# A hybrid decoder trunk: two weight products computed as 2x2 block products in seven multiplications, with the weight sums added up in DRAM

## The chip, the core and the metric

The kernel runs on one core of a Trainium2 chip. The metric is the device time of one execution in microseconds (us). One core has a matrix engine (TensorE, called PE in the profile, with its weight loads as PEld), a vector engine (VectorE, DVE), an activation engine (ScalarE, ACT), a general engine (GpSimd, POOL) and a queue engine (SyncE, SP) which here only starts transfers (DMAs). Each engine works through its own instructions in order and waits on semaphores for the others.

## The reference, cut to what matters

One layer on 512 tokens of width 1024. `h @ W_in` gives the inputs of three branches (a state-space model, a short convolution, a sliding-window attention) and three gates. The part that the change touches comes after them:

```python
merged = (g0 * (y_ssm @ w_branch[0]) + g1 * (y_conv @ w_branch[1]) + g2 * (y_attn @ w_branch[2]))
x = x + merged @ w_out                                    # 1024 x 1024
hf = rms_norm(x, norm_ffn) @ w_ffn_in                     # 1024 x 5632
x = x + (silu(hf[..., :2816]) * hf[..., 2816:]) @ w_ffn_out   # 2816 x 1024
pg = sigmoid(rms_norm(x, norm_ple) @ w_ple_gate)
x = x + pg * (p @ w_ple_proj)
return rms_norm(x, norm_final)
```

All of it is float32. Every product is computed as three products of split numbers: an operand is a high part (`hi`, rounded to the matrix engine's float32r) plus a rest (`lo`), and hi*hi + hi*lo + lo*hi are added up in PSUM.

## The kernel before, in words

**Weight stream.** Every weight matrix is cut into slabs of at most 128x2048 numbers (1 MB), in the order in which they are used. `emit_load` (L179) starts the DMA of a slab on SP into one of two `raw` buffers. A slab has two halves of 1024 columns; `emit_split` (L187) makes a half ready: ACT copies it to `hi` (L206), DVE subtracts to get `lo` (L207, issued up to LAG = 4 ticks later). The halves go round a ring of slots (`hla`, four of them). From the `w_out` stage on the ring has seven slots (`hlb` adds three, L1201). `take` and `group` say which half is wanted now, `retire` that one has been used; both split ahead as far as the ring allows.

**Clock of the program.** `pump()` is called after each triple of matmuls; one call is a tick. `later(d, f)` issues work d ticks on, so that the vector engines' work is put between matmuls. The order on every engine is fixed by this program order; there is no scheduler.

**Stages.** First the start (norm, `p @ w_ple_proj`), then `z_tile` products (8 K-blocks x 3 matmuls of 512 columns for each 128 output columns), the attention beside the convolution, then gates and branch products with the state-space model (SSM) in the background: `ssm_gen` runs four channel tiles, each a chain over PE, ACT, DVE, POOL and small DMAs through DRAM (`su`, `sy`). POOL multiplies in it (L1050, L1063, L1111), and in the convolution (L925 to L929). Then `branch(..., 2)` finishes `merged` tile by tile and splits it into `mh`, `ml` (`split_ap`, L243).

**[token, d] products.** `td_gemm` (L1230) multiplies `merged` by `w_out` and the FFN's hidden tiles by `w_ffn_out`, in three chunks of 8, 8 and 6 hidden tiles (`CHUNKS`, L161). `td_outer_k` (L1218) holds four PSUM banks for the four token tiles and goes over the K-blocks: one weight half serves 2 K-blocks x 4 token tiles x 3 = 24 matmuls. `accum` (L1209) adds each finished bank to the residual `xr`. With a norm behind it (after `w_out` and after the last chunk) the second column half is done token tile by token tile, and `Norm.pre` (L1253) queues square, rstd (POOL), scale (DVE) and the transposes of that tile. The FFN chunks before the products are `z_tile`s: two SiLU tiles and two gating tiles for each pair of hidden tiles, split into `gh`, `gl` (L1320).

The 512 tokens are four tiles of 128; `w_out` has 8 K-blocks, the FFN chunks 8, 8 and 6.

Of the kernel before, what the change touches and what calls it, by code (L numbers as in the profile page):

```python
# [25 lines left out]
WARM = 3  # L26
PREP_RATE = 1.7
# [48 lines left out]
def hybrid_trunk_kernel(  # L76
# [44 lines left out]
    def add_slab(ap, k, n, axis):  # L121
        s = len(slabs)
        slabs.append(dict(ap=ap, k=k, n=n, raw=None))
        cnt = 2 if k * n == 2048 else 1
        for i in range(cnt):
            halves.append(dict(s=s, i=i, cnt=cnt, axis=axis, hl=None))
# [31 lines left out]
    for n in range(2):  # L158
        for kk in range(2):
            add_slab(kn(w_out[0][kk * 512:kk * 512 + 512, n * 512:n * 512 + 512]), 4, 512, "k")  # L160
    CHUNKS = [(0, 8), (8, 8), (16, 6)]  # L161
    for h0, hn in CHUNKS:
        for j in range(h0, h0 + hn, 2):
            for ab in range(2):
                c0 = ab * FFN + j * 128
                add_slab(kn(w_ffn_in[0][:, c0:c0 + 256]), 8, 256, "n")
        for n in range(2):
            for k0 in range(0, hn, 4):
                kq = min(4, hn - k0)
                r0 = (h0 + k0) * 128  # L170
                add_slab(kn(w_ffn_out[0][r0:r0 + kq * 128, n * 512:n * 512 + 512]), kq, 512, "k")
# [5 lines left out]
    state = dict(pump=0, delay=False, split=0, load=0, next=0, top=3, slot=0, pools=[hla] * 4)  # L177

    def emit_load():  # L179
        s = slabs[state["load"]]  # L180
        state["load"] += 1
        t = rawp.tile([128, 2048], F32, tag="raw", name="raw")
        v = t[:, 0:s["k"] * s["n"]].rearrange("p (k n) -> p k n", k=s["k"])
        sp.dma_start(out=v, in_=s["ap"])
        s["raw"] = v

    def emit_split():  # L187
# [5 lines left out]
        k, n, i = s["k"], s["n"], h["i"]  # L193
        if h["cnt"] == 1:
            src = s["raw"]
        elif h["axis"] == "n":
            n //= 2
            src = s["raw"][:, :, i * n:(i + 1) * n]
        else:
            k //= 2  # L200
            src = s["raw"][:, i * k:(i + 1) * k, :]
        pl = state["pools"][state["slot"] % len(state["pools"])]
        state["slot"] += 1
        hi = pl.tile([128, 1024], F32R, tag="hi", name="hi").rearrange("p (k n) -> p k n", k=k)
        lo = pl.tile([128, 1024], F32R, tag="lo", name="lo").rearrange("p (k n) -> p k n", k=k)
# [60 lines left out]
    def pump(tick=True):  # L266
        if tick:
            state["pump"] += 1
            run_due(state["pump"])
# [117 lines left out]
    def prep_gen(tp):  # L387
        # per-channel vectors: ssm_d (4 tiles) and the conv taps (3 x 4 tiles)
# [59 lines left out]
    def prep_fine(tp, lt, ldt, T1, T2, tabs):  # L448
# [73 lines left out]
        # coefficients  # L522
# [85 lines left out]
    # the tensor engine's clock rises only under load  # L608
# [293 lines left out]

    fine.append(dict(gen=attn_fine(), rate=1, credit=0))
# [52 lines left out]
    # chunks of 4 tokens; channels of a group pair and the time in the chunk share the partitions  # L956
    def ssm_gen(ct):
# [69 lines left out]
        # the two row halves of the array write to banks of their own  # L1027
# [117 lines left out]
    def branch(d0, sgs, yh, yl, mode, mh=None, ml=None):  # L1145
        hl = take()
        for i in range(2):
# [8 lines left out]
            if mode == 2:  # L1156
                split_ap(merged[:, d], mh[:, d], ml[:, d])
# [29 lines left out]
    mst = ExitStack()  # L1187
    mhp = open_pool(mst, "mhl", side="right")
    mh = mhp.tile([128, KD, T], F32R, tag="mh", name="mh")
    ml = mhp.tile([128, KD, T], F32R, tag="ml", name="ml")  # L1190
    sg1 = gates()
    branch(0, sg0, yfh, yfl, 2, mh, ml)
    branch(2, sg1, yfh, yfl, 2, mh, ml)
    for d0 in (4, 6):
        branch(d0, gates(), yfh, yfl, 2, mh, ml)
# [7 lines left out]
    state["slot"] = 4  # L1203
# [14 lines left out]
    def td_outer_k(ah, al, kn_, n):  # L1218
        pss = [ps_z() for _ in range(4)]
        for h in range(kn_ // 2):  # L1220
            hi, lo = take()
            for t in range(4):
                for k in range(2):
                    kk = 2 * h + k
                    td_mm(pss[t], ah, al, kk, slice(t * 128, (t + 1) * 128), hi, lo, k, kk == kn_ - 1)
                    pump()
        for t in range(4):
            accum(t, n, pss[t])

    def td_gemm(ah, al, kn_, pre_fn=None):  # L1230
        td_outer_k(ah, al, kn_, 0)
        if pre_fn is None:
            td_outer_k(ah, al, kn_, 1)
            return
        nh = kn_ // 2
        h0 = group(nh)
        for t in range(4):
            ahead()
            ps = ps_z()
            for kk in range(kn_):  # L1240
                hi, lo = halves[h0 + kk // 2]["hl"]
# [180 lines left out]
```

## Time and profile before

| | |
|---|---|
| median of three runs | 894.33 us (893.93 to 896.04) |
| span of the profiled execution, first to last instruction | 892.6 us |
| around the span, to the median of the runs | 1.7 us |
| PE / DVE / ACT / POOL busy | 874.4 / 491.1 / 341.0 / 95.9 us |
| bytes moved by DMA | 107.25 MB |

The page gives the profiled execution no time of its own beside its span. PE's busy time counts overlapped matmuls once; the length shown for a matmul (about 390 ns for 512 columns) is its way through the array, and the distance of two starts is what one costs. "Idle before" is the time that an engine stood still ahead of an instruction, with what released it.

### The profile page before, as it was taken

To read this page: it belongs to the slowest core of one execution; us is meant where nothing else is said; L and a number is where in the kernel's file an instruction comes from. 1 tells how busy PE (TensorE), PEld (TensorE's weight loads), DVE (VectorE), ACT (ScalarE), POOL (GpSimd) and SP (SyncE) were. 2 spreads that over 40 slices of the span, in tenths; PEclk is the share of its full clock that TensorE was granted. 3 is DMA by queue.
4 is the path that set the end of the run, shared out by engine and by line. 5 is a ranking of instruction groups with operands and counts; after the bars stand their busy time and mean duration, and the time that the engine had idled before them with its cause. 6 is when DMAs were issued, how large, how long until landed. Compare 5 with 4: busy or idle time off the path is not lost.

```text
span 892.6 us, 10527 instructions
## 1 busy us (share of the span) xinstructions
PE 874.4 (98%) x4143; PEld 715.2 (80%) x4143; DVE 491.1 (55%) x737; ACT 341.0 (38%) x546; POOL 95.9 (11%) x86
## 2 busy tenths in 40 slices
PE   8999999999999979999999999999999999999997
PEld 6988787877777758888889888888888888888886
DVE  3789698948588585554545433333333333334654
ACT  5665556445443343433334322212222212222533
POOL 1030061713123030000000000000000000000000
PEclk9999999999999989999999999999999999999998
DMA  8756511253634523223813322222225332233002
GB/s 300 216 189 218 195 59 30 66 173 113 178 95 156 156 94 107 95 79 134 284 46 107 130 94 95 95 95 94 95 95 211 99 100 87 72 120 110 29 1 94
DMA packets 84849, 107.25 MB, mean 120 GB/s; under 512 B 6120, under 2 KB 66176, under 8 KB 84288
## 3 DMA queue, kind: packets, MB, share of 16 engines
q1 hardware_dynamic: 84800, 106.59, 36.5%
q8 instruction: 32, 0.52, 0.2%
q14 instruction: 17, 0.14, 0.1%
HBM read 94.83 MB, written 11.55 MB: 119 GB/s over the span
## 4 chain that ended last, share of the span: by engine, by line
PE 77%; DVE 10%; issue 4%; ACT 3%; DMA 3%; SPq 1%; POOL 1%; POOLq 0%; DVEq 0%; ACTq 0%
PE z L248 17%; PE z L249 16%; PE z L250 16%; PE z L1216 8%; PE z L1215 8%; PE z L1214 8%; DVE lo L207 1%; DVE s_t L839 1%; DMA xt<-in_x_dram 1%; PE t L325 1%; DVE s_t L812 1%; DMA raw<-in_w_in_dram 1%; POOL gsw L1063 1%; ACT s_t L826 1%; PE t L1084 1%
## 5 line engine op out<-in xcount | busy, mean ns | idle before, releaser
L248 PE MATMUL z<-h,hi 128*128 128x512 f32 (+1 forms) x776 | 298.6, 385 | 0.0
L207 DVE TENSOR_TENSOR lo<-raw,hi 128x1024 fp32r<-128x1024 f32 x142 | 177.6, 1253 | 216.2 <-ACT hi L206 216.1
L249 PE MATMUL z<-l,hi 128*128 128x512 f32 (+1 forms) x776 | 292.2, 377 | 0.0
L250 PE MATMUL z<-h,lo 128*128 128x512 f32 (+1 forms) x776 | 292.1, 376 | 0.0
L206 ACT CAST hi<-raw 128x1024 fp32r<-128x1024 f32 x142 | 148.2, 1047 | 133.1 <-PE z L1216 87.2
L248 PEld LDWEIGHTS z<-h,hi 128*128 128x128 f32 x776 | 146.8, 189 | 29.9 <-issue 3.7
L250 PEld LDWEIGHTS z<-h,lo 128*128 128x128 f32 x776 | 146.7, 189 | 27.6
L249 PEld LDWEIGHTS z<-l,hi 128*128 128x128 f32 x776 | 147.0, 189 | 24.7
L1214 PE MATMUL z<-hi,gh 128*128 128x512 f32 x176 | 69.5, 395 | 0.0
L1216 PE MATMUL z<-hi,gl 128*128 128x512 f32 x176 | 69.1, 393 | 0.0
L1215 PE MATMUL z<-lo,gh 128*128 128x512 f32 x176 | 69.1, 392 | 0.0
L1265 POOL TENSOR_TENSOR rs<-ms,nhalf 128x1 f32<-128x1 f32 x8 | 4.4, 550 | 487.2 <-DVE ms L1264 487.2
L244 ACT CAST gh<-sil 128x512 fp32r<-128x512 f32 x22 | 13.6, 620 | 86.0 <-DVE sil L1319 86.0
L248 PE MATMUL z<-yh,hi 128*128 128x512 f32 x112 | 45.1, 403 | 0.0
L249 PE MATMUL z<-yl,hi 128*128 128x512 f32 x112 | 44.2, 395 | 0.1
L250 PE MATMUL z<-yh,lo 128*128 128x512 f32 x112 | 44.2, 395 | 0.0
L1310 ACT ACTIVATE sil<-z 128x512 f32<-128x512 f32 x22 | 13.2, 598 | 75.4 <-PE z L250 75.4
L1319 DVE TENSOR_TENSOR sil<-z,sil 128x512 f32<-128x512 f32 x22 | 15.2, 691 | 46.8 <-PE z L250 46.8
L1216 PEld LDWEIGHTS z<-hi,gl 128*128 128x128 f32 x176 | 33.1, 188 | 7.5
L1215 PEld LDWEIGHTS z<-lo,gh 128*128 128x128 f32 x176 | 33.1, 188 | 7.4
L1214 PEld LDWEIGHTS z<-hi,gh 128*128 128x128 f32 x176 | 33.1, 188 | 7.3
L1211 DVE TENSOR_TENSOR xr<-z,xr 128x512 f32<-128x512 f32 x32 | 21.5, 687 | 15.6 <-PE z L1216 15.5
(258 smaller groups left out, 1058.5 us busy)
## 6 DMA issues: line engine op xcount, KB each, us to landing
raw<-in_w_in_dram SPq DMA_DIRECT2D x23, 1024.0 KB, 5.5
raw<-in_w_ffn_in_dram SPq DMA_DIRECT2D x22, 1024.0 KB, 5.2
raw<-in_w_ffn_out_dram SPq DMA_DIRECT2D x10, 1024.0 KB, 5.0
raw<-in_w_branch_dram SPq DMA_DIRECT2D x12, 512.0 KB, 3.4
cs<-tb SPq DMA_DIRECT2D x4, 1024.0 KB, 5.2
raw<-in_w_out_dram SPq DMA_DIRECT2D x4, 1024.0 KB, 5.8
raw<-in_w_ple_gate_dram SPq DMA_DIRECT2D x4, 1024.0 KB, 5.1
xt<-in_x_dram SPq DMA_DIRECT2D x4, 512.0 KB, 9.4
```

The costliest lines, as they stand in the source:

```text
L206: act.copy(out=hi, in_=src)
L207: todo = [lambda: dve.tensor_tensor(lo, src, hi.bitcast(F32), ALU.subtract)]
L244: act.copy(out=hi, in_=src)
L248: pe.matmul(ps, wh, ah, start=first, stop=False)
L249: pe.matmul(ps, wh, al, start=False, stop=False)
L250: pe.matmul(ps, wl, ah, start=False, stop=last)
L1211: dve.tensor_tensor(dst, ps, dst, ALU.add)
L1214: pe.matmul(ps, ah[:, kk, ts], hi[:, k, ns], start=(kk == 0), stop=False)
L1215: pe.matmul(ps, ah[:, kk, ts], lo[:, k, ns], start=False, stop=False)
L1216: pe.matmul(ps, al[:, kk, ts], hi[:, k, ns], start=False, stop=last)
L1310: act.activation(out=s, in_=ps, func=AF.Silu)
L1319: dve.tensor_tensor(sil[i], ps, sil[i], ALU.mult)
```

## The change

`w_out` and each of the three chunks of `w_ffn_out` are taken as 2x2 block products: tokens in two halves of 256, K-blocks in two interleaved halves (even and odd), output columns in two halves of 512. Instead of eight block multiplications there are seven (Strassen's scheme in Winograd's form), each 256 tokens x `kt` K-blocks x 512 columns, with `kt` = 4, 4, 4 and 3. Products that share terms go on adding into the same PSUM bank after it has been read, and each product is added to, or subtracted from, one quarter of `xr`.

*Left sides.* `forms` builds, for a pair of hidden (or merged) tiles, four sums on DVE and splits seven forms of 2x256 or 256 columns into `fh`, `fl`. These take 28 KB a partition each; the ring has four slots instead of seven until the last stage, and `gh`, `gl`, `mh`, `ml` are gone.

*Right sides.* Three of the seven are blocks of the weights, four are sums (`t1` to `t4`), built in DRAM beforehand: per block product eight DMAs on POOL's queue, four copies and four with an add, 1 MB each (0.75 MB in the last chunk), 32 in all. They are issued one every 16 ticks from the start of the attention on; a load that needs them issues what is still missing first.

The gain for the last norm and `pp` (`ppt`) are now loaded when the last stage begins, in a place that the forms left.

```diff
-    for n in range(2):
-        for kk in range(2):
-            add_slab(kn(w_out[0][kk * 512:kk * 512 + 512, n * 512:n * 512 + 512]), 4, 512, "k")
+    A11, A12, A22, FD, S2, S3, S4 = range(7)
+    ORDER = (A11, FD, S2, S4, S3, A12, A22)
+    ORDER_NORM = (A11, FD, S2, S4, A12, S3, A22)
+    def add_block_product(w, r0, kt, order):
+        def blk(h, n):
+            v = w[r0:r0 + 2 * kt * 128, n * 512:n * 512 + 512].rearrange("(i h p) n -> h p i n", h=2, p=128)
+            return v[h]
+        t1, t2, t3, t4 = (dram.tile([128, kt, 512], F32, tag=f"T{len(sums)}_{i}", name="T") for i in range(4))
+        ops = []
+        def op(dst, src, add=False):
+            ops.append(lambda: pool.dma_start(out=dst, in_=src, **(dict(accum_op=ALU.add) if add else {})))
+        op(t1, blk(0, 1))
+        op(t3, blk(0, 1))
+        op(t1, blk(0, 0), True)
+        op(t3, blk(1, 1), True)
+        op(t2, t1)
+        op(t2, blk(1, 1), True)
+        op(t4, t2)
+        op(t4, blk(1, 0), True)
+        sums.append(ops)
+        right = {A11: blk(0, 0), A12: blk(1, 0), A22: t4, FD: t1, S2: t2, S3: t3, S4: blk(1, 1)}
+        for f in order:
+            add_slab(right[f], kt, 512, "k", 16 if len(sums) < 3 else 32)
+    add_block_product(w_out[0], 0, 4, ORDER_NORM)
...
+    for i in (0, 2):
+        sum_ops.extend(f for two in zip(sums[i], sums[i + 1]) for f in two)
     def emit_load():
...
+        while n_sum - len(sum_ops) < s["need"]:
+            sum_ops.popleft()()
...
     def pump(tick=True):
         if tick:
             state["pump"] += 1
+            if state["sums"] and sum_ops and state["pump"] % SUM_EVERY == 0:
+                sum_ops.popleft()()
...
+    def forms(g, i):
+        sums = fmp.tile([128, 4, 256], F32, tag="sums", name="sums")
+        g11, g12, g21, g22 = (g[:, h, o:o + 256] for o in (0, 256) for h in range(2))
+        split_ap(g[:, :, 0:256], fh[:, 0:2, i], fl[:, 0:2, i])
+        dve.tensor_tensor(sums[:, 0], g21, g22, ALU.subtract)
+        dve.tensor_tensor(sums[:, 1], sums[:, 0], g11, ALU.subtract)
+        dve.tensor_tensor(sums[:, 2], g11, g21, ALU.subtract)
+        dve.tensor_tensor(sums[:, 3], g12, sums[:, 1], ALU.add)
+        split_ap(sums, fh[:, 3:7, i], fl[:, 3:7, i])
+        split_ap(g22, fh[:, 2, i], fl[:, 2, i])
...
-    hlb = open_pool(ctx, "hlb", 3)
-    state["pools"] = [hla] * 4 + [hlb] * 3
...
+    PRODUCTS = {A11: (0, True, 1, 0, 0), FD: (1, True, 1, 1, 1), S2: (0, False, -1, 0, 1), S4: (1, False, 1, 0, 1),
+                S3: (0, False, -1, 1, 1), A12: (2, True, 1, 0, 0), A22: (0, False, 1, 1, 0)}
+    def block_product(kt, norm=None):
+        banks = {}
+        for i, f in enumerate(ORDER if norm is None else ORDER_NORM):
+            bk, first, sign, th, n = PRODUCTS[f]
+            if first:
+                banks[bk] = [(ps_t if bk == 2 else ps_z)() for _ in range(2)]
+            for q in range(2):
+                h0 = group(1)
+                if q == 0:
+                    ahead()
+                hi, lo = halves[h0]["hl"]
+                k0, kc = halves[h0]["part"][0:2]
+                for t in range(2):
+                    ps, ts = banks[bk][t], slice(t * 128, (t + 1) * 128)
+                    for k in range(kc):
+                        kk = k0 + k
+                        st = first and kk == 0
+                        last = kk == kt - 1
+                        pe.matmul(ps, fh[:, f, kk, ts], hi[:, k], start=st, stop=False, skip_group_check=True)
+                        pe.matmul(ps, fl[:, f, kk, ts], hi[:, k], start=False, stop=False, skip_group_check=True)
+                        pe.matmul(ps, fh[:, f, kk, ts], lo[:, k], start=False, stop=last, skip_group_check=True)
+                        pump()
+                    if last:
+                        dst = xr[:, 2 * th + t, n * 512:(n + 1) * 512]
+                        dve.tensor_tensor(dst, ps if sign > 0 else dst, dst if sign > 0 else ps,
+                                          ALU.add if sign > 0 else ALU.subtract)
+                        if norm is not None and i in (4, 6):
+                            norm.pre(2 * th + t)
+                retire(h0)
...
-    td_gemm(mh, ml, 8, nf.pre)
+    block_product(4, nf)
...
-                split_ap(sil[i], gh[:, j + i], gl[:, j + i])
+            forms(g, j // 2)
+        block_product(hn // 2, npl if ci == 2 else None)
```

## Rows read from the trace of the kernel before

**Rows 1.** The page: busy time by engine, clock and DMA in 40 slices.
```profile
PE 874.4 (98%) x4143; PEld 715.2 (80%) x4143; DVE 491.1 (55%) x737; ACT 341.0 (38%) x546; POOL 95.9 (11%) x86
PEclk9999999999999989999999999999999999999998
DMA  8756511253634523223813322222225332233002
```
**Rows 2.** Busy time by stretch; columns PE, PEld, DVE, ACT, POOL, clock, DMA share, GB/s.
```profile
200.00:250.00 50.00, 50.00 (x242) 39.06 (x241) 34.81 (x41) 25.47 (x41) 15.08 (x10) 1.00 0.45 133
300.00:350.00 50.00, 45.23 (x201) 34.30 (x200) 30.47 (x38) 16.42 (x24) 7.53 (x5) 0.93 0.46 144
424.00:470.00 46.00, 46.00 (x209) 37.48 (x208) 23.70 (x30) 16.00 (x21) 1.66 (x3) 1.00 0.46 160
560.00:606.00 46.00, 46.00 (x202) 37.54 (x201) 16.35 (x18) 9.79 (x10) 0.00 (x0) 1.00 0.35 112
```
**Rows 3.** Timeline of chunk 0's product: its first matmul, and the first one after it.
```profile
560.76 0.39 PE L1214 MATMUL z<-hi,gh 128*128 128x512 f32 x1
604.93 0.40 PE L248 MATMUL z<-h,hi 128*128 128x512 f32 x1
```
**Rows 4.** Matmuls by line and form: the products with hidden and merged tiles.
```profile
L1214 PE MATMUL z<-hi,gh 128*128 128x512 f32 x176 | 69.5, 395 | 0.0
L1214 PE MATMUL z<-hi,mh 128*128 128x512 f32 x64 | 25.5, 398 | 0.0
```
**Rows 5.** Timeline at the end of chunk 0's last hidden tile, DVE and ACT.
```profile
560.97 0.69 DVE L1319 TENSOR_TENSOR sil<-z,sil 128x512 f32<-128x512 f32 x1 [1.89 <-PE z L250]
561.69 0.62 ACT L244 CAST gh<-sil 128x512 fp32r<-128x512 f32 x1 [3.87 <-DVE sil L1319]
```
**Rows 6.** Instructions on tile xr: shapes from 128 to 512 columns.
```profile
L1345 DVE TENSOR_TENSOR xg<-xr,g x9: 292/692/693, 848.7 to 887.1; 128x512 f32<-128x512 f32 x7, 128x384 f32<-128x384 f32 x1, 128x128 f32<-128x128 f32 x1
```
**Rows 7.** Groups in the stretch 424.0 to 470.3 us (the w_out stage).
```profile
L207 DVE TENSOR_TENSOR lo<-raw,hi 128x1024 fp32r<-128x1024 f32 x9 | 10.8, 1223 | 8.4 <-ACT hi L206 8.4
L1272 DVE SCALAR_TENSOR_TENSOR xn<-xr,rs,g 128x1024 f32<-128x1024 f32 x3 | 3.9, 1285 | 0.8 <-POOL rs L1265 0.7
L245 DVE TENSOR_TENSOR l<-t,h 128x512 fp32r<-128x512 f32 x4 | 2.7, 682 | 0.0
```
**Rows 8.** DMA in the stretch 424 to 438 us: the queue's share, issues to landing.
```profile
q1 hardware_dynamic: 2129, 4.62, 92.3%
xr<-in_x_dram SPq DMA_DIRECT2D x1, 2048.0 KB, 7.9
```
**Rows 9.** Timeline of the w_out stage: xr's load; a slab's load and what waited for it.
```profile
424.14 0.37 SPq L1205 DMA_DIRECT2D xr<-in_x_dram  x1
429.37 0.37 SPq L184 DMA_DIRECT2D raw<-in_w_out_dram  x1
436.55 2.00 ACT L206 CAST hi<-raw 128x1024 fp32r<-128x1024 f32 x2 [6.57 <-DMA raw<-in_w_out_dram]
```
**Rows 10.** The page's DMA issues: KB each, median us to landing.
```profile
raw<-in_w_ffn_out_dram SPq DMA_DIRECT2D x10, 1024.0 KB, 5.0
```
**Rows 11.** Groups in the stretch 88.5 to 423.9 us: triples of 512-column matmuls.
```profile
L248 PE MATMUL z<-h,hi 128*128 128x512 f32 x285 | 117.5, 412 | 0.0
L248 PE MATMUL z<-yh,hi 128*128 128x512 f32 x112 | 45.1, 403 | 0.0
```
**Rows 12.** The chain that ended last, within 297 to 327 us: start, length.
```profile
298.34 3.02 DMA sy<-ys
302.28 7.67 DMA raw<-in_w_in_dram
323.30 2.24 POOL gsw L1063
```
**Rows 13.** Timeline of PE where the SSM's end holds it up.
```profile
324.61 0.80 PE L1082 MATMUL t<-uu,Dg 128*128 128x128 f32 x2 [4.49 <-ACT Dg L1075]
327.94 0.63 PE L250 MATMUL z<-h,lo 128*128 128x512 f32 x1
```

More of the change, by code (lines that the diff above doesn't have):

```diff
@@ L26 @@
 WARM = 3
+SUM_EVERY = 16
 PREP_RATE = 1.7
@@ L119, in hybrid_trunk_kernel, with add_slab @@
     slabs = []
-    def add_slab(ap, k, n, axis):
+    def add_slab(ap, k, n, axis, need=0):
         s = len(slabs)
[L123 to L126, printed above, removed]
+        slabs.append(dict(ap=ap, k=k, n=n, raw=None, need=need))
+        if k * n <= 1024:
+            parts = [(0, k, 0, n)]
+        elif axis == "n":
+            parts = [(0, k, i * (n // 2), n // 2) for i in range(2)]
+        else:
+            k1 = (k + 1) // 2
+            parts = [(0, k1, 0, n), (k1, k - k1, 0, n)]
+        for q in parts:
+            halves.append(dict(s=s, part=q, hl=None))
     def kn(ap):
@@ L176, in hybrid_trunk_kernel @@
     due = {}
-    state = dict(pump=0, delay=False, split=0, load=0, next=0, top=3, slot=0, pools=[hla] * 4)
+    state = dict(pump=0, delay=False, split=0, load=0, next=0, top=3, slot=0, pools=[hla] * 4, sums=False)
+    sum_ops = deque()
+    for i in (0, 2):
+        sum_ops.extend(f for two in zip(sums[i], sums[i + 1]) for f in two)
+    n_sum = len(sum_ops)
     def emit_load():
@@ L901, in attn_fine @@
             yield 1
+    state["sums"] = True
     fine.append(dict(gen=attn_fine(), rate=1, credit=0))
@@ L1230, in td_gemm @@
[L1230 to L1241, printed above, removed]
-                td_mm(ps, ah, al, kk, slice(t * 128, (t + 1) * 128), hi, lo, kk % 2, kk == kn_ - 1)
-                pump()
-                if t == 3 and kk % 2:
-                    retire(h0 + kk // 2, kk == 1)
-            accum(t, 1, ps)
-            pre_fn(t)
+    PRODUCTS = {A11: (0, True, 1, 0, 0), FD: (1, True, 1, 1, 1), S2: (0, False, -1, 0, 1), S4: (1, False, 1, 0, 1),
+                S3: (0, False, -1, 1, 1), A12: (2, True, 1, 0, 0), A22: (0, False, 1, 1, 0)}
@@ L1308, in hybrid_trunk_kernel @@
                     ps = z_tile()
[L1309 to L1311 removed]
+                act.activation(out=g[:, i], in_=ps, func=AF.Silu)
             for i in range(2):
@@ L1318, in hybrid_trunk_kernel @@
                     ps = z_tile()
-                dve.tensor_tensor(sil[i], ps, sil[i], ALU.mult)
-                split_ap(sil[i], gh[:, j + i], gl[:, j + i])
-        if ci == 1:
-            gain = load_gain(norm_final, gainp)
-            sp.dma_start(out=ppt, in_=pp_d.rearrange("(t p) d -> p t d", p=128))
-        if ci == 2:
-            td_gemm(gh, gl, hn, npl.pre)
-        else:
-            td_gemm(gh, gl, hn)
+                dve.tensor_tensor(g[:, i], ps, g[:, i], ALU.mult)
+            forms(g, j // 2)
+        block_product(hn // 2, npl if ci == 2 else None)
     fst.close()
+    fmst.close()
+    hlb = open_pool(ctx, "hlb", 3)
+    state["pools"] = [hla] * 4 + [hlb] * 3
+    state["slot"] = 4
     ep = open_pool(ctx, "ple")
+    gain = load_gain(norm_final, ep)
+    ppt = ep.tile([128, 4, D], F32, tag="ppt", name="ppt")
+    for t in range(4):
+        sp.dma_start(out=ppt[:, t], in_=pp_d[t * 128:(t + 1) * 128, :])
     xg = ep.tile([128, 4, D], F32, tag="xg", name="xg")
```

66 lines of the change are left out of this document (18 added, 48 removed).

## The prediction

> **What bounds the kernel now.** I read the page's busy times first: PE is busy for 98% of the span, DVE for 55%, ACT 38%, POOL 11% [rows 1]. The slices show one dip of the clock and DMA shares from nothing to almost all [rows 1]. So time goes away where matmuls go away, as long as the others keep up. The stretches say where that holds [rows 2]: in the `w_out` stage and in chunk 0's product PE is busy throughout at full clock; between 300 and 350 us it stands still for 4.8 us, on a chain of the SSM through POOL, ACT and small DMAs [rows 2, 12, 13]. What a 512-column matmul costs is the distance of starts: chunk 0's product runs from 560.76 to 604.93 us with 8 x 4 x 2 x 3 = 192 of them, 0.230 us each [rows 3]. Counts agree with the code: 64 x 3 for `w_out`, 176 x 3 for the FFN [rows 4].
>
> **What goes.** A block product with `kt` = 4 has 7 x 4 x 2 x 3 = 168 matmuls for 192; three such save 72. With `kt` = 3 it has 126 for 144, which saves 18. Together 90 x 0.230 = 20.7 us, all on the engine that sets the time. Tiling and operand types stay, so I keep the pace. This is the only gain.
>
> **What comes, part by part.**
>
> *Starts of the products.* Before, the last hidden pair was first needed at K-block 6, behind 3 halves of 24 matmuls. Now a product's first form has only four K-blocks, half of the tokens at a time: the last pair's `lo` is first used by the 17th matmul, 16 x 0.230 = 3.7 us after the start, at 564.4 in chunk 0. Its chain there: the gating product on DVE ends at 561.66, the cast on ACT at 562.31 [rows 5]; meanwhile DVE makes four sums of 256 columns. These have no row; between 0.29 (128 columns) and 0.69 (512) [rows 6] I take 0.42, so they end at 563.34, and the subtraction (0.69) at 564.0. That is in time by 0.4 us, and late by 0.8 if one weight subtraction of 1.22 us [rows 7] stands in between. I take 0.5 us for each of four starts, 2 us; range 0 to 6.
>
> *DVE and ACT elsewhere.* The forms add, for each of 15 pairs, 4 x 0.42 us and about 0.9 us of splitting on DVE; that lies under four products of 5.5 us a pair. In a product with `kt` = 4 a slab lasts 24 x 0.230 = 5.5 us; DVE owes it two subtractions of 1.22 and two updates of `xr` of 0.69, 3.8 us: it keeps up. ACT's load is smaller.
>
> *The two products with a norm.* Now two token tiles are done after the fifth product and two after the last; formerly they came one after another. A tile costs DVE 1.29 + 2 x 0.68 + about 0.15 = 2.8 us [rows 7]. In the last two products of `w_out` DVE owes 2 x 3.8 + 2 x 2.8 = 13.2 us in 11.0; in the last chunk, whose slabs last 18 x 0.230 = 4.1 us, 2 x 3.3 + 5.6 = 12.2 in 8.3. That is 2.2 and 3.9 us too much. Halves are subtracted about one half (2.8 us) ahead, which covers part. I take half of the sum, 3 us; range 0 to 8. Also S3 and A22 follow each other in one bank, so A22 waits for the update (0.69) of a tile that ended six matmuls (1.4 us) before: covered if DVE is free, and part of the same term if not.
>
> *Four slots, and halves that last half as long.* A half now feeds 12 matmuls (2.8 us), formerly 24. In steady state a slab's `raw` buffer is freed about 2 us after the first half of the slab behind it has begun; from there a load of 5.0 us [rows 10] and a cast and subtraction of 2.3 leave about 3.5 us until the half is due. So the FFN chunks hold the pace. Four slots are no limit for the `z_tile` products either: until 424 us the ring had four, and PE was busy for 50.00 of 50 us between 200 and 250 [rows 2].
>
> *The `w_out` stage* is another matter. Its DMA engines are busy for 92% between 424 and 438 us, with 4.62 MB moved [rows 8]: `xr` (2 MB, 7.9 us from its issue at 424.14), the gain and the weights. A slab issued at 429.37 is cast at 436.55, 7.2 us later [rows 9]. Seven slots of 5.5 us each stood in front of it; now there are four of 2.8 us. The fourth slab (S4, half 6) would be issued and land about when that one did, and it is due at 424 + 6 x 2.76 = 440.5, with cast and subtraction ready at about 439: just. The first update of `xr` waits from 429.5 to 432.0 for the load, and keeps one subtraction behind it (ready 434, due 435). Sums come on top. Ticks between the start of attention and 424 us are 285 + 112 = 397 [rows 11], which issues 24 of 32; about 3.5 fall into this stage. A copy of 1 MB at 4.62 MB in 14 us is 3.1 us of all DMA engines, an add reads twice, so 6.2 at most: 16 us of transfers, in a stage of 39 us that already needs 9.5 MB, 29 us. That is 45 for 39; 2 MB less may be held at its end, since what follows eats half as fast (6 us). So it nearly fits, in lumps. I take 4 us; range 0 (all in the gaps) to 10 (each sum in front of a load, 3.5 x 3.1).
>
> *Sums beside attention and SSM.* 24 DMAs on POOL's queue in 335 us, one each 13.5 us. The first 16 are done long before `w_out` asks, so nothing is issued in a burst, and an add finds the DMA that it waits for issued two steps (27 us) earlier. The `z_tile`s bear a slower load: 11 us a slab. The SSM's end does not: it is a chain in which a store of `sy` takes 3.02, a load of weights 7.67 and POOL 2.24 us [rows 12], and PE stands still for 4.49 us at its end and then runs matmuls of 0.63 us [rows 13] while the clock mean is 0.93 [rows 2]. On the last 57 us of it fall about four sums. How long POOL is held by such an issue no row shows, since it issues none; SP's takes 0.37 us [rows 9], POOL's longest piece here 2.24. At the low end all of it lies beside POOL's gaps: 0. At the high end four issues of 2.24 us and two chain transfers lengthened by a 1 MB transfer of 3.1 each: 15 us. I take the value near SP's row, 4 x 0.4, plus half a collision, 3 us.
>
> The rows have DMAs of SP alone (one queue holds the 92%). The Trainium skill, DMA: Bandwidth & Descriptors, section "Issuing engines are not separate DMA queues", says that transfers issued by different engines run on the same 16 DMA engines and interleave. By it a sum is not free because POOL issues it, and the terms for the `w_out` stage and the SSM stand; were the queues apart, both would shrink to POOL's time, and the sum to 14 us gained. No run here shows which.
>
> *The last stage* loads gain and `ppt` (2.5 MB) at its start, at the rate above 7.6 us; they are first used 5.5 us in, and the wait holds only DVE, with work that PE needs 11 us in. 0.
>
> **The sum.** 2 + 3 + 4 + 3 = 12 us against 20.7: 8.7 us gained. The profiled execution's span is 892.6 us, so 883.9; with the 1.7 us that lie between it and the median of the runs (894.33), 885.6. I say 885.5.
>
> **The rivals.**
>
> *A, forecast:* as above, 879 to 892; its own range from half to one and a half times the costs (6 to 18 us). Chance 0.45.
>
> *B, everything is covered:* only the starts cost, 1 to 4 us; 892.6 - 20.7 + 2 + 1.7 = 875.6. For it: PE is never kept waiting by weights in the FFN, and DVE has 45% free. Against it: the 92% of the DMA engines in the `w_out` stage. Chance 0.20.
>
> *C, the sums hold up the SSM's chain:* slower than before. Each sum that falls on it keeps POOL, or a transfer that the chain waits for, and PE stands still at the end, at the lower clock after it. It decides from the point where the four sums on the last 57 us cost more than 20.7 - 9 = 11.7 us, about 3 us each. If each costs a 1 MB load's 5.0 us and another 2 us of POOL, 28 us: 894.3 - 20.7 + 9 + 28 = 911; halfway, 900. For it: the chain ran through POOL and DMA already. Against it: POOL has gaps, and before 266 us the chain was PE's own. Chance 0.22.
>
> *D, the block products starve:* weights come at the pace of a loaded DMA, 7.2 us a slab [rows 9] for 5.5. `w_out` alone would lose 7 x 1.7 = 12 us, with adds in FFN chunk 0 another 5: 894.3 - 20.7 + 17 + 5 = 895.6, no change. For it: rows 8; against it: the chunks' 5.0 us. Chance 0.13. That the change does not do what it says is out: the matmul count is in the code.
>
> **How the numbers follow.** About 0.3% (2.7 us) is what a measurement tells from no change here, so faster means below 891.6 and slower above 897.0. Faster: 0.43 of A, all of B, 0.02 of D: 0.65. Slower: nearly all of C and 0.03 of D: 0.23. Same: 0.12. The range leaves out the lowest of B and the upper third of C: 874 to 903; A's own is 879 to 892.
>
> **What would show it.** 462 and 168 matmuls in the products for 528 and 192; chunks 0 and 1 at 39 to 40 us for 44.2. A `w_out` stage of about 43 to 44 us instead of 46.2 (16 transposes of the norm are in it), with PE waiting for `lo` (DVE) or for raw. PE's wait for `Dg` or for POOL near 325 us grown by about 3 us. The prediction is wrong if PE's stops between 100 and 340 us grow by more than 10 us, or if the product stages come out above 46 us.

## The result, and the profile after

The changed kernel takes 901.62 us (median of five runs, 897.75 to 902.23), the kernel before, run beside it, 895.79 (893.93 to 896.21). The ratio is 1.0067, with a 95% interval of 1.0046 to 1.0089: slower by 0.7%, where 1% faster was forecast. That is 16 us away from the forecast of 885.5, though inside the range. In the profiled executions the span grew from 892.6 to 899.6 us.

The page of the changed kernel: busy time, clock and DMA in 40 slices, and the two DMA queues (packets, MB, the time that their packets took as a share of 16 engines' span).

```profile
PE 861.2 (96%) x4053; PEld 701.3 (78%) x4053; DVE 562.4 (63%) x862; ACT 375.5 (42%) x587; POOL 124.5 (14%) x118
PEclk9999999999999988999999999999999999999899
DMA  8658542497777539995657833264332452225702
q1 hardware_dynamic: 85168, 118.39, 39.9%
q0 software_dynamic: 10240, 31.46, 15.2%
```

Against [rows 1] PE has 90 matmuls and 13.2 us of work less, and yet the span is longer, so PE stands still for longer. The digits say where to look: DMA shares of 7 to 9 tenths in slices 9 to 13 and 16 to 18 (180 to 405 us), where 2 to 6 stood, and a lower clock in slices 15 and 16, before in 15 alone. (The last stage has a lower digit of its own, in slice 38 now and in slice 40 before.) The DMA engines move 31.46 MB of sums on the queue of POOL.

Where it went, by stages (from the first matmul of one stage to the first of the next, in the traces of four kernels; `e1` leaves the sums out, `e12` is the last version below):

| us | before | after | e1 | e12 |
|---|---|---|---|---|
| start to the convolution's branch products | 204.23 | 205.47 | 204.37 | 203.10 |
| SSM, to its last branch product | 136.98 | 148.05 | 137.38 | 137.34 |
| other gates and branches | 82.74 | 83.09 | 82.74 | 81.60 |
| `w_out` and its norm | 46.21 | 43.10 | 43.17 | 43.29 |
| FFN tiles, chunk 0 | 90.60 | 93.80 | 90.10 | 90.09 |
| product, chunk 0 | 44.17 | 39.20 | 39.20 | 39.20 |
| FFN tiles, chunk 1 | 88.30 | 87.07 | 87.07 | 87.07 |
| product, chunk 1 | 44.22 | 39.20 | 39.20 | 39.20 |
| FFN tiles, chunk 2 | 66.07 | 65.31 | 65.30 | 65.30 |
| product, chunk 2, with a norm | 35.12 | 37.61 | 36.95 | 33.19 |
| last stage | 53.96 | 57.70 | 57.62 | 56.52 |

The products give what they should (-3.1, -5.0, -5.0). The SSM takes 11.1 us more, the FFN's start 3.2, the last product and the last stage together 6.2. Within the SSM the loss lies in two places: 5.7 us in the gates up to 280 us (69.26 us long before, 74.93 now) and 5.2 in the last gates before its end (21.95 and 27.18).

PE's waits in the trace of the changed kernel (start, length, instruction, and in brackets the idle time before it and what ended that). The first three lie in the SSM, the next two in and behind `w_out`, the last two in the last product and behind it.

```profile
218.46 0.46 PE L1119 MATMUL t<-uu,Dg 128*128 128x128 f32 x2 [1.23 <-POOL gsw L1100]
271.50 0.67 PE L1071 MATMUL t<-uu,ET 64*128 64x128 f32 x4 [2.88 <-ACT ET L1031]
336.07 0.80 PE L1119 MATMUL t<-uu,Dg 128*128 128x128 f32 x2 [8.87 <-ACT Dg L1112]
472.71 0.47 PE L1287 MATMUL z<-hi,fh 128*128 128x512 f32 x1 [1.24 <-DVE xr L1293]
486.89 0.79 PE L361 MATMUL t<-cst,xn 128*128 128x128 f32 x4 [1.99 <-DVE ms L1314]
833.36 0.77 PE L1287 MATMUL z<-hi,fh 128*128 128x512 f32 x1 [3.50 <-DVE xr L1293]
853.77 0.66 PE L361 MATMUL t<-cst,xn 128*128 128x128 f32 x4 [2.59 <-DVE l L279]
```

The wait for `Dg` was 4.49 us [rows 13] and is 8.87. What grew beside it is the DMAs: issues by kind on the page of the changed kernel (KB each, median us from issue to landing), and the same kinds before.

```profile
raw<-in_w_in_dram SPq DMA_DIRECT2D x23, 1024.0 KB, 7.4
T<-in_w_out_dram POOLq DMA_DIRECT2D x6, 1024.0 KB, 9.6
sy<-ys SPq DMA_DIRECT2D x32, 32.0 KB, 6.6
```

```profile
raw<-in_w_in_dram SPq DMA_DIRECT2D x23, 1024.0 KB, 5.5
sy<-ys SPq DMA_DIRECT2D x32, 32.0 KB, 1.7
```

A store of 32 KB lands after 6.6 us instead of 1.7, and the SSM has 32 of them. SP is held, too. Its issue of one channel tile's eight stores, before and in the changed kernel (start, length):

```profile
259.91 3.61 SPq L1092 DMA_DIRECT2D sy<-ys  x8
```

```profile
262.20 8.01 SPq L1129 DMA_DIRECT2D sy<-ys  x8
```

The chain that ended last ran through PE's matmuls from 255 to 270 us before; now it runs through one load of weights (start, length):

```profile
258.65 11.24 DMA raw<-in_w_in_dram
```

The stretches (columns as in [rows 2]; the SSM now ends at 353.5 us, before at 341.2) show the same: from 300 to 350 us PE is busy for 40.75 us instead of 45.23 at a mean clock of 0.86 instead of 0.93, with the DMA engines at 0.63 instead of 0.46; from 350 on they are at 0.96, and there, with no chain of small stores, PE loses nothing.

```profile
200.00:250.00 50.00, 48.77 (x239) 37.64 (x238) 34.73 (x42) 24.30 (x39) 15.52 (x13) 1.00 0.77 226
300.00:350.00 50.00, 40.75 (x183) 30.39 (x182) 30.43 (x39) 18.49 (x31) 12.71 (x10) 0.86 0.63 170
350.00:400.00 50.00, 50.00 (x219) 40.82 (x218) 22.23 (x28) 14.20 (x20) 8.97 (x10) 1.00 0.96 253
```

POOL's issues of sums show the order that the program gives, not its pace: the first at 66 us, ahead of the stretch from 88.5 us on in which I had counted ticks, and nine between 363 and 400 us. POOL stops for an earlier step of a sum seven times, 35.5 us in all, and the first of these stops is the one shown below at 370.39 us, behind the SSM: in the SSM no multiplication of POOL stood behind a stop for a sum.

```profile
66.19 0.90 POOL L183 DMA_DIRECT2D T<-in_w_out_dram  x1
363.65 3.92 POOL L183 DMA_DIRECT2D T<-in_w_ffn_out_dram  x4
370.39 1.17 POOL L183 DMA_DIRECT2D T<-in_w_ffn_out_dram  x1 [2.83 <-DMA T<-in_w_ffn_out_dram]
```

Chunk 0's product, its first matmul and the first one after it, as [rows 3]: 39.20 us for 168 matmuls, 0.233 each.

```profile
573.51 0.40 PE L1287 MATMUL z<-hi,fh 128*128 128x512 f32 x1
612.71 0.39 PE L282 MATMUL z<-h,hi 128*128 128x512 f32 x1
```

### The profile page after: what moved, and what is told of

Same layout as the page of the kernel before. It is cut to its first block, busy times and chain, and to the rows that moved or that the text cites. A ratio compares the mean times of both kernels' runs of the same rounds, so it can differ in the third digit from the quotient of the medians.

```text
span 899.6 us, 10656 instructions
## 1 busy us (share of the span) xinstructions
PE 861.2 (96%) x4053; PEld 701.3 (78%) x4053; DVE 562.4 (63%) x862; ACT 375.5 (42%) x587; POOL 124.5 (14%) x118
## 3 DMA queue, kind: packets, MB, share of 16 engines
q0 software_dynamic: 10240, 31.46, 15.2%
HBM read 138.09 MB, written 43.00 MB: 201 GB/s over the span
## 4 chain that ended last, share of the span: by engine, by line
PE 65%; DVE 15%; DMA 8%; issue 4%; ACT 4%; POOL 3%; SPq 1%; POOLq 0%; DVEq 0%; ACTq 0%
PE z L282 15%; PE z L284 15%; PE z L283 15%; PE z L1287 4%; PE z L1288 4%; PE z L1289 4%; DVE lo L241 3%; DMA cs<-tb 2%; DVE s_t L875 2%; PE z L1263 1%; PE z L1262 1%; PE z L1261 1%; DVE s_t L848 1%; DMA raw<-in_w_in_dram 1%; PE t L361 1%
## 5 line engine op out<-in xcount | busy, mean ns | idle before, releaser
L241 DVE TENSOR_TENSOR lo<-raw,hi 128x1024 fp32r<-128x1024 f32 (+1 forms) x168 | 204.8, 1223 | 146.2 <-ACT hi L240 146.1
L240 ACT CAST hi<-raw 128x1024 fp32r<-128x1024 f32 (+1 forms) x168 | 171.1, 1029 | 178.9 <-DMA raw<-in_w_in_dram 49.7
L1287 PE MATMUL z<-hi,fh 128*128 128x512 f32 x180 | 72.7, 404 | 4.7 <-DVE xr L1293 4.7
L1288 PE MATMUL z<-hi,fl 128*128 128x512 f32 x180 | 72.1, 400 | 0.0
L1289 PE MATMUL z<-lo,fh 128*128 128x512 f32 x180 | 71.9, 399 | 0.0
L1361 DVE TENSOR_TENSOR g<-z,g 128x512 f32<-128x512 f32 x22 | 15.2, 692 | 62.0 <-PE z L284 62.0
L282 PE MATMUL z<-yh,hi 128*128 128x512 f32 x112 | 45.2, 404 | 0.6 <-ACT yh L278 0.6
L1287 PEld LDWEIGHTS z<-hi,fh 128*128 128x128 f32 x180 | 34.2, 190 | 13.2 <-ACT hi L240 3.9
L1288 PEld LDWEIGHTS z<-hi,fl 128*128 128x128 f32 x180 | 34.3, 191 | 8.5 <-DVE fl L279 0.8
L1289 PEld LDWEIGHTS z<-lo,fh 128*128 128x128 f32 x180 | 34.3, 190 | 8.2
L1353 ACT ACTIVATE g<-z 128x512 f32<-128x512 f32 x22 | 13.2, 600 | 55.9 <-PE z L284 55.9
## 6 DMA issues: line engine op xcount, KB each, us to landing
T<-in_w_ffn_out_dram POOLq DMA_DIRECT2D x12, 1024.0 KB, 10.1
```

Of the source, the lines that this page charges most:

```text
L240: act.copy(out=hi, in_=src)
L241: todo = [lambda: dve.tensor_tensor(lo, src, hi.bitcast(F32), ALU.subtract)]
L282: pe.matmul(ps, wh, ah, start=first, stop=False)
L1287: pe.matmul(ps, fh[:, f, kk, ts], hi[:, k], start=st, stop=False, skip_group_check=True)
L1288: pe.matmul(ps, fl[:, f, kk, ts], hi[:, k], start=False, stop=False, skip_group_check=True)
L1289: pe.matmul(ps, fh[:, f, kk, ts], lo[:, k], start=False, stop=last, skip_group_check=True)
```

## Experiments

Each ratio is to the kernel before on the same chip, with its 95% interval. Spans are those of one profiled execution each, so a difference of two spans is the rougher figure. The theory: the sums hold up the SSM. Open was by what: POOL's time at their issue, the traffic of 32 MB, or the adding. A rival: the block products themselves lose the time.

**Without the sums.** No sum is built; the slabs that would hold one are loaded from plain blocks of the weights, so traffic of the loads, matmuls and forms stay and the values of the sums are left out.

```diff
-        op(t1, blk(0, 1))
...
-        op(t4, blk(1, 0), True)
...
-        right = {A11: blk(0, 0), A12: blk(1, 0), A22: t4, FD: t1, S2: t2, S3: t3, S4: blk(1, 1)}
+        right = {A11: blk(0, 0), A12: blk(1, 0), A22: blk(1, 1), FD: blk(0, 1), S2: blk(0, 1), S3: blk(0, 1), S4: blk(1, 1)}
```

> Leaves out all 32 sum DMAs; the four sum slabs of each block product are loaded from plain weight blocks of the same size, so the products with sums are not formed. Theory: the sums beside attention and SSM cost the 12 us by which PE's stretch from 205 us to the SSM's end grew (69.3 to 74.9 and 22.0 to 27.2 us); without them that stretch is as before (PE idle of about 4.5 us at its end for 8.9) and the time is 889 to 891 us. Rival (the SSM lost time to the re-laid memory and the four-slot ring, or to chance): the stretch stays longer by 8 us or more and the time is 898 or more. Both: the ends of the two products with a norm keep their 16 us (product 3 about 37.6 us, last stage about 57.7).

Measured: 884.95 us, ratio 0.9908 (0.988 to 0.9936), below the 889 to 891 expected. The sums cost 14 us by the two ratios (0.0159 of 895) and 16.5 by the spans of the two traces (899.6 and 883.1). The table says where: 1.1 before the SSM, 10.7 in it, 3.7 at the FFN's start. But without them the ratio gives 8 us, and the spans 9.5, and not 20.7; the waits at the last product are still there, as PE's waits of this kernel show (one in the SSM, one in the last product):

```profile
325.25 0.80 PE L1111 MATMUL t<-uu,Dg 128*128 128x128 f32 x2 [5.00 <-ACT Dg L1104]
817.85 0.47 PE L1279 MATMUL z<-hi,fh 128*128 128x512 f32 x1 [3.75 <-DVE xr L1285]
```

**POOL's issue alone.** The 32 DMAs on POOL's queue with their waits, but 16 numbers of each row of 512; their results are not used, and plain blocks are loaded as in the first experiment.

```diff
-            ops.append(lambda: pool.dma_start(out=dst, in_=src, **(dict(accum_op=ALU.add) if add else {})))
+            ops.append(lambda: pool.dma_start(out=dst[:, :, 0:16], in_=src[:, :, 0:16], **(dict(accum_op=ALU.add) if add else {})))
...
```

> As e1_no_sums, but POOL issues the 32 DMAs at the same ticks with the same waits and as many pieces, each of 64 bytes in place of 2 KB, so 32 times fewer bytes; the result of these is not used. Theory (the transfers' traffic stretches the SSM's small transfers and the weight loads): as e1_no_sums within 2 us, 889 to 892. Rival (POOL is held by the issues, 0.5 to 1.2 us each, and its multiplications in the SSM come late): as the changed kernel, 898 to 902.

Measured: 885.73 us, 0.9908 (0.9885 to 0.9931), as without any. The wait for `Dg` is 4.67 us. That POOL issues 32 such DMAs costs nothing measurable here. Its stops between two steps are shorter than with whole transfers; but in the changed kernel they lie behind the SSM, as shown above.

```profile
324.92 0.80 PE L1119 MATMUL t<-uu,Dg 128*128 128x128 f32 x2 [4.67 <-ACT Dg L1112]
```

**Traffic on another queue.** 32 plain copies of the same sizes into buffers that nobody reads, issued by ACT; blocks are loaded as above.

```diff
-            ops.append(lambda: pool.dma_start(out=dst, in_=src, **(dict(accum_op=ALU.add) if add else {})))
+            ops.append(lambda: act.dma_start(out=dst, in_=src))
...
```

> As e1_no_sums, but with 32 plain copies of 1 MB (0.75 MB) from DRAM to DRAM issued at the same ticks by ACT's queue: traffic without POOL and without adds. Theory (traffic): the SSM stretch grows again by 6 to 12 us against e1_no_sums, sy's stores take 4 us or more for 1.7; time 895 to 902. Rival (POOL held, or the adds as such): as e1_no_sums, 889 to 892.

Measured: 888.32 us, 0.9934 (0.9912 to 0.9956). The expectation was missed: copies of the same bytes cost 2 us by the ratios against the kernel without sums (the two intervals overlap), 5 by the spans (888.2 and 883.1), not the 6 to 12 expected. The copies do touch the SSM's stores (3.4 us to landing, 1.7 before) and its last gates stretch (24.81 us; 22.36 without sums, 27.18 with).

```profile
sy<-ys SPq DMA_DIRECT2D x32, 32.0 KB, 3.4
```

**Copies for adds, on POOL's queue.** Everything stays, the loads from the sums too; only the 16 adding DMAs become plain copies, so the values of the sums are left out.

```diff
-            ops.append(lambda: pool.dma_start(out=dst, in_=src, **(dict(accum_op=ALU.add) if add else {})))
+            ops.append(lambda: pool.dma_start(out=dst, in_=src))
```

> The changed kernel with each of the 16 adding DMAs turned into a plain copy of the same bytes, on POOL's queue at the same place (the sums are not formed). Theory (an add costs the DMA engines more than a copy, and that is what separates the changed kernel from e3_act_copies): the SSM stretch shrinks to that of e3 or near it, time 888 to 893. Rival (the number of transfers on POOL's queue and their bunching matter, adds cost like copies): as the changed kernel, 898 to 902.

Measured: 888.21 us, 0.9932 (0.9906 to 0.9958), as expected. Against the kernel without sums copies cost 2 us by the ratios and 3 by the spans; that half of them add costs 12 more by the ratios (0.0135 of 895) and 13.5 by the spans (899.6 and 886.1). The page of this kernel:

```profile
q0 software_dynamic: 6400, 31.46, 10.2%
T<-in_w_out_dram POOLq DMA_DIRECT2D x6, 1024.0 KB, 6.2
sy<-ys SPq DMA_DIRECT2D x32, 32.0 KB, 3.6
```

The same 31.46 MB take 10.2% of 886.1 us, 90.4 us, or 2.8 us of all 16 engines for each of the 32 copies. With 16 adds it was 15.2% of 899.6, 136.7 us: less 45.2 for 16 copies, an add takes 5.7 us, twice a copy. That is the price I had estimated for transfers by themselves; what it does to others was the part that I had not. The adds also come in more packets, 10240 for 6400. That is not what costs: ACT's copies moved the same bytes in 15872 packets, for 10.4% of 888.2 us.

```profile
q10 hardware_dynamic: 15872, 31.46, 10.4%
```

**Fewer sums, later.** Only chunks 0 and 1 are block products; `w_out` and the last chunk are as before, and the sixteen sums come after the SSM.

```diff
-SUM_EVERY = 16
+SUM_EVERY = 12
...
+        if hn == 8:
+            add_block_product(w_ffn_out[0], h0 * 128, hn // 2, ORDER)
...
-    state["sums"] = True
     fine.append(dict(gen=attn_fine(), rate=1, credit=0))
...
+    state["sums"] = True
+    mst = ExitStack()
```

> Block products only for the first two FFN chunks; w_out and the last chunk as in the kernel before (the ring has four slots until the last chunk, then seven); 16 sums, issued from the end of the SSM on. Theory (the loss lies in the SSM and in the two products with a norm; the other two give 5 us each and about 1 us in the stages behind them): 894.3 - 10 - 2 = 882 to 885 us, SSM stretch as before. Rival (the block products gain nothing when the whole is taken together): 892 or more.

Measured: 883.86 us, 0.9893 (0.9852 to 0.9934): the two products' 10 us, and no loss in the SSM. The FFN's tiles of chunk 0 took 94.52 us for 90.60, the sums being issued at 469 to 487 us, where those slabs are loaded.

**Sums moved by ticks.** First with three block products (`w_out`, chunks 0 and 1): `w_out`'s sums start with the attention, the others after the SSM, one every 6 ticks. Then with all four, the 24 others from the SSM's end on. The edit shown is the first one's; the second sets 32 where it has 24.

```diff
-SUM_EVERY = 16
+SUM_EVERY = 6
...
-            if state["sums"] and sum_ops and state["pump"] % SUM_EVERY == 0:
+            if len(sum_ops) > n_sum - state["sums"] and state["pump"] % SUM_EVERY == 0:
...
-    state["sums"] = True
+    state["sums"] = 8
     fine.append(dict(gen=attn_fine(), rate=1, credit=0))
...
+    state["sums"] = 24
     fmst = ExitStack()
...
```

> Block products for w_out and the first two FFN chunks, the last chunk as in the kernel before; w_out's eight sums issued during attention, the sixteen others from the end of the SSM on, one every 6 ticks; none beside the SSM. Theory: e1_no_sums without what its last chunk and last stage lose (5.5 us): about 880, if the sums are hidden beside attention and branches; 879 to 884. Rival (1 MB sums cost wherever they lie): 888 or more.

> The changed kernel whole, only the sums moved in time: w_out's eight during attention, none beside the SSM, the 24 others from its end on, one every 6 ticks. Theory (the loss against e1_no_sums is the place, beside the SSM's chain): the SSM stretch is back (69.3 and 22.0 to 22.7 us), time 885 to 889. Rival (the bytes cost wherever they lie): 896 or more.

Measured: 907.73 us, 1.0158 (1.0126 to 1.0189), and 920.89 us, 1.0299 (1.0267 to 1.033): both missed, slower than the change itself. A tick fixes only which POOL instruction stands ahead of an issue. With none ahead that waits, POOL issues at once: in the second kernel two sums at 67 us and two more by 79 us, and the DMA share is 0.95 from 66 to 110 us (5 to 6 tenths before [rows 1]) and PE waits 9.85 us; later ones in a row up to and into the `w_out` stage, which has a share of 0.96. That stage takes 52.84 us in the first kernel and 61.49 in the second.

```profile
67.03 1.67 POOL L183 DMA_DIRECT2D T<-in_w_out_dram  x2
```

```profile
106.44 0.45 PE L844 MATMUL t<-KH,Q 128*128 128x128 f32 x1 [9.85 <-DVE mx L849]
449.89 0.79 PE L1289 MATMUL z<-hi,fh 128*128 128x512 f32 x1 [4.58 <-ACT fh L279]
```

```profile
66.00:110.00 44.00, 34.15 (x154) 28.17 (x153) 29.31 (x49) 18.95 (x29) 5.37 (x5) 0.88 0.95 273
441.70:503.00 61.30, 48.17 (x185) 36.12 (x184) 37.30 (x48) 22.22 (x29) 7.74 (x9) 0.89 0.96 274
```

**Sums tied to data.** Three block products again. `w_out`'s eight sums are issued after the SSM; each chunk's eight stand behind a small POOL instruction that reads the chunk's first gating product, so POOL can't run ahead.

```diff
...
+            if j == 0 and (ci < 2):
+                gate = sm.tile([128, 1], F32, tag="gate", name="gate")
+                pool.tensor_tensor(gate, g[:, 1, 0:1], nhalf, ALU.mult)
+                for _ in range(8):
+                    sum_ops.popleft()()
...
```

> Block products for w_out and the first two FFN chunks as in e6_three_products, but the sums moved again: w_out's eight after the SSM (nothing beside attention, SSM or the w_out stage), each FFN chunk's eight behind a small POOL instruction that waits for the chunk's first hidden pair, so POOL cannot run ahead. Theory (an adding DMA costs nothing beside a stage in which the loads have slack, and a lot beside one that runs at the DMA's or a chain's pace): attention, SSM and w_out stages as in e1_no_sums, 879 to 883. Rival (each sum costs PE time wherever it lies): 888 or more.

Measured: 878.70 us, 0.982 (0.9805 to 0.9835), as expected (879 to 883). The sums of chunk 0 lie in its tiles now, with the DMA engines at 0.89, and PE is busy throughout at full clock:

```profile
492.00:550.00 58.00, 58.00 (x258) 48.04 (x257) 26.53 (x35) 18.83 (x25) 7.25 (x8) 1.00 0.89 238
```

**The wait of the last product.** Is DVE overloaded there, or is it its order? First, on the kernel without sums, every second weight subtraction in the later products of a norm goes to POOL.

```diff
-        todo = [lambda: dve.tensor_tensor(lo, src, hi.bitcast(F32), ALU.subtract)]
+        eng = pool if state["lo"] and state["split"] % 2 else dve
+        todo = [lambda: eng.tensor_tensor(lo, src, hi.bitcast(F32), ALU.subtract)]
...
+            state["lo"] = norm is not None and i >= 3
```

> e1_no_sums with every second weight subtraction of the two products with a norm, from the fourth block on, given to POOL instead of DVE. Theory (DVE owes more than it can do in the last two blocks, so the update of xr that A22's first matmul waits for comes late): the waits of 1.3 and 3.75 us before A22 fall under 1 us, the last chunk takes 33 to 34 us for 36.95, time 880 to 883. Rival (the wait is the bank's, S3 and A22 following each other, whatever DVE owes): both waits stay, 884 to 886.

Measured: 888.89 us, 0.9947 (0.993 to 0.9964): nothing gained over 884.95. The wait before the last form stays at 3.95 us, and `w_out` takes longer (47.73 us). But the run does not answer the question, since DVE is not relieved: in the last product it has 38 instructions instead of 41 and is busy for 28.25 us instead of 28.83, in `w_out` 33.85 instead of 33.74. POOL needs 2.4 to 2.8 us for each such subtraction, and an instruction of DVE that runs beside one takes longer: in `w_out` a norm's scale takes 3.38 us instead of 1.29. The first two lines are from the last product, the others from `w_out`:

```profile
813.62 5.21 POOL L234 TENSOR_TENSOR lo<-raw,hi 128x1024 fp32r<-128x1024 f32 x2 [335.26 <-PE t L1283]
824.01 0.52 PE L1281 MATMUL z<-hi,fh 128*128 128x512 f32 x1 [3.95 <-DVE xr L1287]
458.25 2.36 POOL L234 TENSOR_TENSOR lo<-raw,hi 128x1024 fp32r<-128x1024 f32 x1
458.31 3.38 DVE L1317 SCALAR_TENSOR_TENSOR xn<-xr,rs,g 128x1024 f32<-128x1024 f32 x1 [0.67 <-POOL rs L1310]
```

The order has to be changed by itself. DVE in the changed kernel, just before A22's first matmul at 833.36:

```profile
828.65 1.29 DVE L1322 SCALAR_TENSOR_TENSOR xn<-xr,rs,g 128x1024 f32<-128x1024 f32 x1 [0.74 <-POOL rs L1315]
829.85 0.15 DVE L1314 TENSOR_SCALAR ms<-ss 128x1 f32<-128x1 f32 x1
830.73 1.29 DVE L1322 SCALAR_TENSOR_TENSOR xn<-xr,rs,g 128x1024 f32<-128x1024 f32 x1 [0.73 <-POOL rs L1315]
831.93 0.69 DVE L241 TENSOR_TENSOR lo<-raw,hi 128x512 fp32r<-128x512 f32 x1
832.53 1.28 DVE L1293 TENSOR_TENSOR xr<-xr,z 128x512 f32<-128x512 f32 x2
```

Two norms, each standing 0.7 us for POOL's `rs`, are queued ahead of the update of `xr` that must read S3's bank before A22 may write it. Second, then, on the kernel without sums: the last product's scale four ticks later, and the transposes behind it one tick later. What DVE does stays the same; only its order changes.

```diff
...
-    npl = Norm(load_gain(norm_ple[0], gainp))
+    npl = Norm(load_gain(norm_ple[0], gainp), (1, 3, 8, 10, 11))
```

> e1_no_sums with the last norm's scale on DVE four ticks later, so that it stands behind the update of xr that A22's first matmul waits for, not ahead of it. Theory (the 3.75 us wait before A22 is DVE's order: two norm chains, each standing for POOL's rs, in front of the update): the wait falls under 1.5 us, the last chunk from 36.95 to 33.5 to 35 us; the time by up to 2.5 us, less if the norm's end comes later by as much. Rival (DVE simply owes too much): the wait stays above 2.5 us, 884 to 886.

Measured: 880.30 us, 0.9838 (0.9823 to 0.9852), 4 us less than without by the spans (879.0 and 883.1), 6 by the ratios, more than the 2.5 expected. The wait is 0.73 us, the last product 33.26. The update now stands ahead of the two scales. So it was the order: in the six kernels with the old order and DVE's work as in the change the wait is 3.29 to 4.01 us, in the two with the new order 0.73 and 0.65.

```profile
814.33 1.28 DVE L1285 TENSOR_TENSOR xr<-xr,z 128x512 f32<-128x512 f32 x2
815.53 2.48 DVE L1314 SCALAR_TENSOR_TENSOR xn<-xr,rs,g 128x1024 f32<-128x1024 f32 x2
815.16 0.47 PE L1279 MATMUL z<-hi,fh 128*128 128x512 f32 x1 [0.73 <-DVE xr L1285]
```

**Both together.** All four block products as in the change, each one's sums placed as in "Sums tied to data" (`w_out`'s behind the SSM, the last chunk's behind its first gating product), and the later scale.

> The changed kernel whole (four block products), with the sums placed as in e9_three_hidden (the last chunk's also behind its predecessor's first pair or its own) and the scale as in e10_scale_later. Theory: e1_no_sums's 885 within 2 us, less what e10 gains: 882 to 887, and 2 to 5 us above e9_three_hidden, since the last chunk's block product and norm give nothing. Rival: 896 or more (sums cost wherever they lie).

Measured: 878.01 us, 0.9804 (0.977 to 0.9838): 1.6% to 2.3% faster than before, and below the 882 to 887 expected, which had counted less for the later scale and nothing for the faster branch products (under "Open"). It is no slower than any other kernel here, though its interval holds that of the three products. Its sums take as much of the DMA engines as the change's (15.6% of 875.9 us), and the wait for `Dg` is 5.22 us:

```profile
q0 software_dynamic: 10240, 31.46, 15.6%
```

```profile
324.09 0.80 PE L1119 MATMUL t<-uu,Dg 128*128 128x128 f32 x2 [5.22 <-ACT Dg L1112]
```

## Why the prediction was wrong

**The step that failed is "Sums beside attention and SSM", put at 3 us (0 to 15).** It measured 12.3 (1.2 ahead of the SSM and 11.1 in it), inside its range and four times its value, and the sums cost 3.2 more at the FFN's start. It was right that about four sums fall on the last 57 us of the SSM and that its chain suffers there. But half of the SSM's loss, 5.7 us, came before 281 us, where I had counted on slack ("The `z_tile`s bear a slower load: 11 us a slab"): one load took 11.24 us there, and PE stopped for 2.88 us behind it at 271.50. And the price was wrong in kind. I priced an issue, near SP's 0.37 us, "plus half a collision". The issue costs nothing that shows (885.73 us with it, 884.95 without); the collision is all of it. And I took a collision as one transfer that lengthens two others, while beside transfers that keep all 16 engines at work for 5.7 us each many others took longer: stores went from 1.7 to 6.6 us, a load of the chain to 11.24, and SP needed 8.01 us for eight stores, so that it issued later what came behind. Rival C named the place and the sign, 900 at its halfway point; its "2 us of POOL" was not there.

The prediction had set a mark for this, PE's stops between 100 and 340 us growing by more than 10. It was reached, narrowly: PE stands still for 7.2 of these 240 us before and for 17.6 after, 10.5 more (columns as in [rows 2], before and after):

```profile
100.00:340.00 240.00, 232.84 (x1122) 182.42 (x1122) 180.53 (x303) 113.00 (x225) 74.45 (x57) 0.98 0.37 113
100.00:340.00 240.00, 222.36 (x1067) 172.99 (x1068) 172.29 (x295) 108.97 (x219) 88.33 (x73) 0.97 0.61 167
```

Of the 11.1 us in the SSM itself 8.6 are such stops; in the other 2.5 PE is busy longer with the same products, at a mean clock of 0.94 instead of 0.98.

**"One each 13.5 us"** was wrong too. I read ticks as times. They are places in an order, and an engine with nothing to wait for comes there early: 27 of the 32 were issued ahead of the `w_out` stage, where I had counted 24; the two experiments that moved the sums by ticks show what it can cost. By their ratios they are 14 and 27 us slower than the kernel before.

**The two products with a norm** were the second miss: 3 us (0 to 8), and 0 for the last stage. Each product is compared with its stage before, less 24 or 18 matmuls at 0.230: `w_out` 43.10 for 40.7, the last product 37.61 for 31.0, the last stage 57.70 for 53.96. That is 12.8 us, and 12.1 without the sums. I summed what DVE owes in a window and let work ahead cover half; what counted in the last product was that two chains with a wait for POOL stood in front of one update (3.7 us of that product, by the experiment with the later scale). I had written "A22 waits for the update ... covered if DVE is free", and counted it into that sum instead of asking what DVE's queue holds at that moment. The last stage begins with two tiles' norms instead of one; in the last version its first transposes still wait 1.68 and 0.88 us. That this beginning is the cause of the 3.7 us there, no run shows.

**The DMA term of the `w_out` stage**, 4 us, was not paid there (43.10 us with the sums, 43.17 without), because all of the sums but one had been issued ahead of it or came after it. The mechanism is real where they do fall there (52.84 and 61.49 us). What was paid came one stage later, and the trace shows through which transfer. The one add that falls into the stage (0.75 MB, issued at 469.47) takes 8.1 us to land. The load of weights that SP issues beside it at 472.03 lands after 8.3 us, without the sums after 5.0. ACT waits 4.13 us for it, DVE behind ACT, the norm comes late, and PE waits 1.99 us at 486.89:

```profile
raw<-in_w_ffn_in_dram SPq DMA_DIRECT2D x1, 1024.0 KB, 8.3
480.43 1.05 ACT L240 CAST hi<-raw 128x1024 fp32r<-128x1024 f32 x1 [4.13 <-DMA raw<-in_w_ffn_in_dram]
```

In the first 10 us of the FFN's tiles PE's mean clock is 0.88, in the next 10 us 0.95; without the sums it is 1.00 in both. The stop and 1.7 us more of busy time are the 3.7 us by which the stage differs from that without sums (90.10 us).

**Right:** 20.7 us of matmuls go. A chunk's product takes 39.20 us ("39 to 40") and PE does not wait in it, so the starts cost 0 where I took 2; the pace is 0.233 us instead of 0.230, 0.5 us a product. Four slots are enough. DVE and ACT carry the forms beside the tiles (87.07 us for 88.30). `w_out` came out at 43.10, inside "43 to 44", though for another reason than given. On the rule cited, that DMAs of different engines run on the same 16 DMA engines: copies issued by ACT stretch the stores that SP issues from 1.7 to 3.4 us, those issued by POOL to 3.6. The Trainium skill, DMA: Bandwidth & Descriptors, section "Issuing engines are not separate DMA queues", agrees with that; that POOL issued the sums did not make them free.

The sum, in measured numbers: -20.7 for the matmuls; +12.3 ahead of and in the SSM, +3.2 at the FFN's start, +12.8 for norms, +1.0 for the pace, -2.0 in the tiles of chunks 1 and 2, +0.4 elsewhere: the 7.0 us by which the span grew. With the first miss alone put right (3 for 12.3) the span would have changed by -2.3 us, with the norms alone at their 3 by -2.8: about no change either way, and it took both to be slower.

**Open.** The cost of adding rests on the 12 to 13.5 us between two kernels that differ in it alone; that an add reads its target before it writes would explain twice the time of a copy, but no run separates reading from writing, and the profile's page counts the same bytes for both kernels (138.09 MB read from DRAM, 43.00 written). In the two versions with sums tied to data the branch products take 5.44 us a tile instead of 5.59, some 2 us in all, for which I have no cause.

## What to carry to other kernels

A transfer that nobody waits for is not free: ask which small transfers run beside it, and what chain hangs on those, and put it where only large loads with slack run (0.89 of the DMA engines in an FFN stage cost PE nothing; at 0.63, in the SSM's last part, PE was busy for 40.75 of 50 us instead of 45.23). A place in program order is no time; an engine that should issue late needs an operand that comes late. Where a product's bank is reused, look at what stands ahead of its reader in the engine's queue, not at how much that engine has to do.

## What the runs showed of the hardware that was not expected

An adding DMA from DRAM to DRAM took 5.7 us of all 16 DMA engines for 1 MB, a copy 2.8, and the DMAs of such a sum that read a block of 1 MB, adds among them, landed after a median of 9.6 to 10.1 us, copies alone after 6.2 to 6.7. Beside such adds a store of 32 KB took 6.6 us instead of 1.7, and SP needed 8.01 us to issue eight instead of 3.61. POOL's subtraction of 128x1024 numbers took 2.4 to 2.8 us, DVE's 1.22 [rows 7]; and a scale of DVE took 3.38 us while one of POOL's subtractions ran, 1.29 otherwise.
